# Where a gate is multiplied in, and which queue copies a key: a two-block transformer kernel on one core

## The chip, the cores and the metric

The kernel runs on one core of a Trainium2 chip. The metric is the time of one execution in microseconds of device time: 2701.52 us as the median of three runs, from 2699.83 to 2702.96. A core has a matrix engine (PE in the profile; its weight loads are PEld), a vector engine (DVE), a scalar engine (ACT), GpSimd (POOL) and a sync engine (SP) that issues DMAs. Each engine works through its own list of instructions strictly in order. POOL can issue DMAs as well: these run on a queue of their own, `software_dynamic` in the profile, while those of SP run on `hardware_dynamic`. POOL does not read PSUM, the memory into which the matrix engine writes.

## The reference

Two blocks are computed in float32. The first has a hybrid mixer (dilated attention and an mLSTM), a cross attention and a mixture of 16 experts over 512 tokens. The second has two layers over two streams, the 512 latent tokens `x` and 256 context tokens `xc`, with one set of weights for both. Cut to what matters here:

```python
for l in range(DEPTH_2):                      # 2 layers
    ctx_out = l < DEPTH_2 - 1                 # the context stream is carried on only after layer 0
    sh1, sc1, g1, sh2, sc2, g2 = split(silu(c) @ w_ada[l] + b_ada[l])            # latent
    sh1c, sc1c, g1c, sh2c, sc2c, g2c = split(silu(c_ctx) @ w_ada[l] + b_ada[l])  # context
    o, oc = token_mixers(modulate(x, sh1, sc1), modulate(xc, sh1c, sc1c), ...)
    x = layer_norm(ALPHA * x + g1 * (o @ w_out[l]), ...)
    x = layer_norm(ALPHA * x + g2 * swiglu(modulate(x, sh2, sc2), ...), ...)
    if ctx_out:
        xc = layer_norm(ALPHA * xc + g1c * (oc @ w_out[l]), ...)
        xc = layer_norm(ALPHA * xc + g2c * swiglu(modulate(xc, sh2c, sc2c), ...), ...)
```

The gates `g1`, `g2` and their context forms are vectors of 1024 numbers, one for each output column. So `g * (o @ W)` can be had in two ways: the gate multiplies the columns of W, or it multiplies the product. `token_mixers` holds a neighbourhood attention (NA, 6 heads), a gated linear attention (GLA) and a grouped-query attention (GQA, 2 key heads).

## The kernel before

Products are made of float32 numbers split into two parts: every weight chunk (128 partitions x 1024 numbers, 512 KB) is loaded by SP into `raw`, rounded by ACT into `w_h` (line 350), and DVE writes the rest `w_l = raw - w_h` (line 351). The matrix engine then does three products for each pair of tiles (lines 340 to 344). `wchunk` (line 383) is that chain. If it is given a `row`, POOL multiplies `raw` by it in place first, at line 387, between the landing of the load and ACT.

`proj_tok` (line 394) walks over column halves of 512 and over chunks of a weight, holds one PSUM tile (`pj`) for each 128 tokens, and calls `evac` for each tile at the end. In `out_proj` (line 2076) and `ffn` (line 2097) `evac` adds the PSUM tile onto the residual `x` on DVE (lines 2088 and 2107). The context stream has two token tiles (`nt` = 2), the latent stream four. In the context's layer 0 the gates go into the weights with `row=`: 8 chunks of `w_out` with `g1b`, 22 chunks of the second FFN weight with `g2b`. For latents, `g1b` multiplies the PSUM tile in `out_proj` (lines 2084 to 2087), and `g2b` goes into the weights of the FFN (22 chunks in each of two layers).

The order of the work: the first block runs until about 520 us. Then come the 16 experts, and beside them, as a foreground with the experts pumped in between, the context's layer 0 (to about 1200 us). A context stream has its own small rings (two `raw` buffers, two split buffers, two `pj` tiles; line 1184). Then the context's layer 1, which gives only keys, values and states, then the two latent layers, about 1290 to 2000 us and 2000 to 2707 us. The program is handed to a scheduler that sets the order on each engine at build time; nothing is reordered on the chip.

In attention each key tile needs a second copy of its rows on the other 64 partitions. `dup_k` (line 530) makes four DMAs of 64 partitions for each key tile, all issued by SP: `nak_h`, `nak_l` for NA (called through `stack_k` at line 1590, three pairs of heads per layer) and `gak_h`, `gak_l` for GQA (line 1790). In a latent layer of 512 tokens one such copy moves 128 KB. POOL issues there the loads of the NA bias tiles, `nab` (line 1621), each when the tile's earlier content has been read, and ACT negates them on landing (line 1622). POOL also computes part of the rotary embedding, `gu` (line 1763).

Of the kernel before, what the change touches and what calls it, by code (L numbers as in the profile page):

```python
# [9 lines left out]
F32 = mybir.dt.float32  # L10
# [5 lines left out]
OP = mybir.AluOpType  # L16
# [4 lines left out]
P = 128  # L21
# [11 lines left out]
ALPHA = (2.0 * 2) ** 0.25  # L33
# [202 lines left out]
def f32(ap):  # L236
    return ap.bitcast(F32)
# [22 lines left out]
class Kern:  # L260
# [259 lines left out]
        for h in range(2):  # L520
            self.split(HL(vd(dst[0:64, h]), vd(dst[64:128, h])), vs(ps[64 * h:64 * h + 64]), scale)

    def stack_k(self, k, ps):

        for h in range(2):
            r = slice(64 * h, 64 * h + 64)
            self.split(k[r, h], ps[r])
        self.dup_k(k)

    def dup_k(self, k):  # L530
        for t in (k.hi, k.lo):
            for h in range(2):
                self.nc.sync.dma_start(out=f32(t[64 - 64 * h:128 - 64 * h, h]), in_=f32(t[64 * h:64 * h + 64, h]))

    def scores(self, sc, q, segs):

# [1048 lines left out]
    def na_kq(self, f, l, hT, T, W, lat, full, pool, g, d):  # L1585

        nc = self.nc
        blk = lambda t: t.rearrange("p (b r c) -> p b r c", b=4, c=16)
        k = g["k"] = self.hl_tile(pool, [P, 2, T], "nak", f"nak{f % 2}")
        yield from self.feat_pieces(hT, T, W[:, 384 + f * P:384 + (f + 1) * P], lambda ps: self.stack_k(k, ps[:, :T]))  # L1590
        if not lat:
            d["na_k"].append(self.spill(k, f"nakc{l}{f}"))
        if not full:
            return
        q = g["q"] = pool.tile([P, 2, T], F32R, name="naq", tag=f"naq{f % 2}")

        def ev_q(ps):
            if not lat:
                return self.stack_q(q, ps[:, :T], 0.125)

            for h in range(2):
                t = q[0:64, h], q[64:128, h]
                src = ps[64 * h:64 * h + 64].rearrange("p (r b c) -> p b r c", b=4, c=16)
                nc.scalar.activation(blk(t[0]), src, AF.Copy, scale=-0.125)
                for b in range(4):
                    bs = slice(b * P, (b + 1) * P)
                    nc.vector.scalar_tensor_tensor(out=t[1][:, bs].rearrange("p (r c) -> p r c", c=16), in0=src[:, b],
                                                   scalar=-0.125, in1=f32(t[0][:, bs]).rearrange("p (r c) -> p r c", c=16),
                                                   op0=OP.mult, op1=OP.subtract)
        yield from self.feat_pieces(hT, T, W[:, f * P:(f + 1) * P], ev_q)  # L1610
# [89 lines left out]
    def gqa(self, l, hT, T, W, ctxd, full, d, keep, pool, between, woven):  # L1700


        nc, A = self.nc, self.A
        nt = T // P
        lat = ctxd is not None
# [20 lines left out]
        kS = self.hl_tile(keep, [P, 2, T], "gak")  # L1726
        if full:
            qS = keep.tile([P, 3, 2, T], F32R, name="gaq")
        if lat:
# [4 lines left out]
            for w, nm in ((qw, "q"), (kw, "k")):  # L1734
# [6 lines left out]
                for bb in range(2):  # L1741
                    for aa in range(2):
                        nc.gpsimd.tensor_tensor(out=t4[:, :, aa, bb, :], in0=s4[:, :, aa, bb, :],
                                                in1=w4[:, aa, 1 - bb, :].unsqueeze(1).to_broadcast([P, 4, 16]), op=OP.mult)
                tabs.append((tcs, tsn))
        for i in range(nt):
            t = sq()
            nc.vector.tensor_tensor(out=t, in0=qk[:, i], in1=r[:, i, :].unsqueeze(2).to_broadcast([P, nh, 64]), op=OP.mult)
            f = pool.tile([P, nh, 64], F32, name="gf", tag="gf", bufs=2)
            if lat:  # L1750
                u = pool.tile([P, nh, 64], F32, name="gu", tag="gu", bufs=1)
            for h0, h1, w, ti in ((0, nq, qw, 0), (nq, nh, kw, 1)):
                n = h1 - h0
# [3 lines left out]
                if lat:  # L1757
# [4 lines left out]
                    for bb in range(2):  # L1762
                        nc.gpsimd.tensor_tensor(out=u5[:, :, :, bb, :], in0=s5[:, :, :, 1 - bb, :],
                                                in1=t5[:, :, bb, :].unsqueeze(1).to_broadcast([P, n, 2, 16]), op=OP.mult)
# [3 lines left out]
            f, t = (t, f) if lat else (f, t)  # L1768
# [16 lines left out]
            for h in range(2):  # L1785
# [1 line left out]
                if full:  # L1787
                    self.split(HL(qS[0:64, :, h, ts], qS[64:128, :, h, ts]), tp[r2, 0:384].rearrange("p (k t) -> p k t", t=P))
                self.split(kS[r2, h, ts], tp[r2, (nb - 1) * P:nb * P])
        self.dup_k(kS)  # L1790
        vs = lambda t, hh, j: t[:, j, 64 * hh:64 * hh + 64]
        if not lat:
            d["ga_k"], d["ga_v"] = self.spill(kS, f"gakc{l}"), self.spill(v, f"gavc{l}")
# [267 lines left out]
    def behind_input(self, hT, pool, works):  # L2061

        t = pool.tile([P, 1], F32, name="bhd", tag="bhd", bufs=1)
        with self.tc.issue_after(self.nc.gpsimd.tensor_copy(t, f32(hT.lo[:, KT - 1, T1 - 1:T1])).ins):
            for f in works:
                f()

    def call(self, f):
        if f is not None:
            f()  # L2070
# [5 lines left out]
    def out_proj(self, l, oT, nt, x, g1b, pool, tile_done):  # L2076

        nc = self.nc
        W = self.A["w_out_2"][l]
        stats = {}  # L2080

        def ev(i, c0, n, ps):
            s = slice(c0, c0 + n)
            if nt == 4:
                t = pool.tile([P, 512], F32, name="gps", tag="gps", bufs=1)
                nc.vector.tensor_tensor(out=t, in0=ps, in1=g1b[:, s], op=OP.mult)
                ps = t
            nc.vector.scalar_tensor_tensor(out=x[:, i, s], in0=x[:, i, s], scalar=ALPHA, in1=ps[:, :n], op0=OP.mult, op1=OP.add)
            self.ln_stats(stats, x, i, c0)
            if c0 + n == D:  # L2090
                return tile_done(i, stats[i])
        if nt < 4:
            return self.proj_tok(oT, nt, W, lambda *a: self.call(ev(*a)), row=g1b)
        self.proj_tok(oT, nt, W[:, 0:512], ev)
        self.proj_last(oT, nt, W, ev, pool, KT, None, (512,))

    def ffn(self, l, hT, T, x, g2b, pool, tile_done):

        nc, A = self.nc, self.A
        nt = T // P  # L2100
        Wi, Wo = A["w_ffn_in_2"][l], A["w_ffn_out_2"][l]
        nf = FF // P
        stats = {}

        def ev(i, c0, n, ps):
            s = slice(c0, c0 + n)
            nc.vector.tensor_tensor(out=x[:, i, s], in0=x[:, i, s], in1=ps[:, :n], op=OP.add)  # L2107

        def ev_last(i, c0, n, ps):
            ev(i, c0, n, ps)  # L2110
            self.ln_stats(stats, x, i, c0)
            if c0 + n == D:
                return tile_done(i, stats[i])
        f0, begun = 0, []
        for fg in (4, 4, 4, 4, 2, 4):
            gT = self.hl_tile(pool, [P, 4, T], "wk", bufs=3 if nt == 4 else 2)
            if f0 == 0 and nt == 4:
                begun = self.in_halves(hT, T, [Wi[:, c:c + P] for c in (0, FF, P)], lambda: self.sc("fab"))
            for f in range(fg):
                ab = []  # L2120
                for z in (0, FF):
                    if begun:
                        ab.append(begun.pop(0))
                        continue
                    c0 = z + (f0 + f) * P
                    w = self.wchunk(Wi[:, c0:c0 + P], KT, P)
                    ab.append(self.sc("fab")[:, 0:T])
                    self.mm3(ab[-1], [(w[:, k, :], hT(k)) for k in range(KT)])
                s = pool.tile([P, T], F32, name="fs", tag="fs", bufs=2)
                nc.scalar.activation(s, ab[0], AF.Silu)  # L2130
                nc.vector.tensor_tensor(out=s, in0=s, in1=ab[1], op=OP.mult)
                self.split(gT[:, f, :], s)
            rows = Wo[f0 * P:(f0 + fg) * P, :]
            f0 += fg
            if f0 < nf or nt < 4:
                self.proj_tok(lambda k: gT[:, k, :], nt, rows, ev if f0 < nf else lambda *a: self.call(ev_last(*a)), kt=fg, row=g2b)
            else:
                self.proj_last(lambda k: gT[:, k, :], nt, rows, ev_last, pool, 4, g2b, (0, 512), lag=2)

# [228 lines left out]
```

## Time and profile before

| what | value |
|---|---|
| median of three runs | 2701.52 us |
| profiled execution, own time | 2709.36 us |
| its span, first to last instruction | 2707.6 us |
| PE, DVE, ACT, POOL busy | 93%, 64%, 47%, 15% |
| mean granted PE clock | 0.963 of full speed |

The profile shows one execution. Busy shares are averages over stages with different limits, so a stage is read by itself with the view of stretches, and a wait by the view that says which instruction ended it. Matmuls overlap each other, so the time of one in a row is longer than its share of the engine. `[1.31 <-DVE w_l L351]` at the end of a row says that the engine had been idle for 1.31 us and that the DVE instruction of line 351 that writes `w_l` let it go.

### The profile page before, as it was taken

How to read it: one execution, taken by the hardware profiler on the slowest of the kernel's cores; microseconds unless marked ns; L12 is line 12 of the kernel's file. 1: busy time of each engine (PE TensorE's matmuls, PEld its weight loads, DVE VectorE, ACT ScalarE, POOL GpSimd, SP SyncE). 2: the span in 40 equal slices, each digit the busy share in tenths (PEclk: the TensorE clock that was granted, in tenths of full speed). 3: DMA queues.
4: the chain of work that ended last, by engine and by line, in shares of the span. 5: the costliest groups of instructions: out<-in, count | busy, mean ns of one | idle time of the engine just before them, and what ended most of it. 6: DMA issues, size and time to landing. Idle time of an engine off the chain costs nothing. (4 is left out here: it accounts for less than half of the span.)

```text
span 2707.6 us, 35926 instructions
## 1 busy us (share of the span) xinstructions
PE 2515.4 (93%) x13176; PEld 1963.8 (73%) x13176; DVE 1725.2 (64%) x3117; ACT 1281.9 (47%) x2389; POOL 418.7 (15%) x304
## 2 busy tenths in 40 slices
PE   8999899798889999988998999999989899999997
PEld 5547575676667888877786588888868666888886
DVE  3346646797687787778786665444567776644446
ACT  4344444576655555556656642222266574422221
POOL 1100000201022121022220023111141200411101
PEclk9999899899999999998999999999989999999999
DMA  7765357588777888767254123333323524233331
GB/s 276 208 203 160 117 192 244 159 268 282 250 241 234 268 276 276 252 222 220 81 156 137 69 87 122 96 94 94 104 86 96 146 82 133 71 101 93 94 93 63
DMA packets 355157, 436.54 MB, mean 161 GB/s; under 512 B 20384, under 2 KB 228128, under 8 KB 354976
## 3 DMA queue, kind: packets, MB, share of 16 engines
q1 hardware_dynamic: 350560, 416.90, 49.1%
q0 software_dynamic: 4416, 17.30, 1.8%
q8 instruction: 105, 1.72, 0.3%
q14 instruction: 76, 0.62, 0.1%
HBM read 387.21 MB, written 38.01 MB: 157 GB/s over the span
## 5 line engine op out<-in xcount | busy, mean ns | idle before, releaser
L351 DVE TENSOR_TENSOR w_l<-raw,w_h 128x1024 fp32r<-128x1024 f32 (+2 forms) x530 | 714.5, 1359 | 465.8 <-ACT w_h L350 456.6
L350 ACT CAST w_h<-raw 128x1024 fp32r<-128x1024 f32 (+2 forms) x530 | 527.5, 1007 | 855.6 <-PE pj L343 272.2
L343 PE MATMUL fab<-hTf_h,w_h 128*128 128x512 f32 (+1 forms) x1104 | 386.2, 351 | 4.1 <-ACT hTf_h L514 3.4
L343 PE MATMUL fab<-hTf_h,w_l 128*128 128x512 f32 (+1 forms) x1104 | 386.7, 351 | 0.5 <-DVE w_l L351 0.4
L343 PE MATMUL fab<-hTf_l,w_h 128*128 128x512 f32 (+1 forms) x1104 | 386.2, 350 | 0.2
L387 POOL TENSOR_TENSOR raw<-raw,g2b 128x1024 f32<-128x1024 f32 x66 | 172.3, 2617 | 708.5 <-DMA raw<-in_w_ffn_out 615.1
L343 PE MATMUL pj<-w_l,hT_h 128*128 128x512 f32 (+3 forms) x608 | 229.8, 379 | 14.1 <-DVE w_l L351 14.1
L343 PE MATMUL pj<-w_h,hT_h 128*128 128x512 f32 (+3 forms) x608 | 222.2, 378 | 14.9 <-ACT w_h L350 9.9
L343 PEld LDWEIGHTS fab<-hTf_h,w_h 128*128 128x128 f32 x1104 | 208.9, 190 | 37.2 <-ACT hTf_h L514 4.5
L343 PEld LDWEIGHTS fab<-hTf_h,w_l 128*128 128x128 f32 x1104 | 209.2, 190 | 32.8 <-DVE w_l L351 1.2
L343 PEld LDWEIGHTS fab<-hTf_l,w_h 128*128 128x128 f32 x1104 | 209.2, 190 | 32.2 <-DVE hTf_l L515 0.6
L343 PE MATMUL pj<-w_h,hT_l 128*128 128x512 f32 (+3 forms) x608 | 225.0, 372 | 0.0
L343 PE MATMUL pj<-w_h,wk_h 128*128 128x512 f32 x376 | 148.5, 401 | 7.9 <-DVE x L2107 4.9
L343 PEld LDWEIGHTS pj<-w_h,hT_h 128*128 128x128 f32 x608 | 118.6, 197 | 45.8 <-ACT w_h L350 13.4
L343 PEld LDWEIGHTS pj<-w_l,hT_h 128*128 128x128 f32 x608 | 120.5, 198 | 42.4 <-DVE w_l L351 18.3
L343 PE MATMUL pj<-w_l,wk_h 128*128 128x512 f32 x376 | 150.0, 400 | 1.1 <-DVE w_l L351 0.9
L343 PE MATMUL pj<-w_h,wk_l 128*128 128x512 f32 x376 | 147.3, 399 | 1.2 <-DVE wk_l L351 1.2
L343 PE MATMUL pf<-hT_h,w_h 128*128 128x512 f32 (+3 forms) x376 | 133.4, 356 | 10.2 <-DVE nak_l L351 3.1
L343 PEld LDWEIGHTS pj<-w_h,hT_l 128*128 128x128 f32 x608 | 120.3, 198 | 22.0 <-issue 5.2
L343 PE MATMUL pf<-hT_h,w_l 128*128 128x512 f32 (+3 forms) x376 | 131.2, 350 | 0.0
L343 PE MATMUL pf<-hT_l,w_h 128*128 128x512 f32 (+3 forms) x376 | 131.2, 350 | 0.0
L577 ACT COPY pT<-ptp 128x512 f32<-128x512 f32 (+3 forms) x184 | 88.5, 497 | 53.5 <-PE ptp L575 52.4
(598 smaller groups left out, 4840.7 us busy)
## 6 DMA issues: line engine op xcount, KB each, us to landing
raw<-in_w SPq DMA_DIRECT2D x192, 512.0 KB
raw<-in_w_ffn_in SPq DMA_DIRECT2D x132, 512.0 KB
raw<-in_w_ada SPq DMA_DIRECT2D x96, 512.0 KB
raw<-in_w_in SPq DMA_DIRECT2D x76, 512.0 KB
raw<-in_w_ffn_out SPq DMA_DIRECT2D x66, 512.0 KB
raw<-in_w_out SPq DMA_DIRECT2D x32, 512.0 KB
yd<-ysb SPq DMA_DIRECT2D x16, 512.0 KB
raw<-in_w_in SPq DMA_DIRECT2D x16, 384.0 KB
```

The lines of the kernel that those rows point to most:

```text
L343: self.nc.tensor.matmul(out, lhsT=l, rhs=r, start=first and k == 0 and i == 0, stop=last and k == n - 1 and i == 2, **kw)
L350: nc.scalar.copy(out=hl.hi, in_=src)
L351: nc.vector.tensor_sub(out=hl.lo, in0=src, in1=f32(hl.hi))
L387: self.nc.gpsimd.tensor_tensor(out=raw, in0=raw, in1=row.unsqueeze(1).to_broadcast([P, kt, n]), op=OP.mult)
L577: nc.scalar.copy(out=pT()[:, slice(b0, b0 + bb), ts], in_=tp[:, :bb * P].rearrange("p (b t) -> p b t", t=P))
```

## The change

Two things are moved. In the context's layer 0 the gates no longer multiply weight chunks: `out_proj` multiplies the PSUM tile for both streams, and `ffn` does it for the context alone. For that a new function `times` has DVE write `ps * g` to a tile `gps` in SBUF, of which there is one. And the copies of the latent keys, in NA and in GQA, are issued by POOL; those of the context stay with SP.

```diff
-    def stack_k(self, k, ps):
+    def stack_k(self, k, ps, eng=None):
...
-        self.dup_k(k)
-
-    def dup_k(self, k):
+        self.dup_k(k, eng)
+
+    def dup_k(self, k, eng=None):
         for t in (k.hi, k.lo):
             for h in range(2):
-                self.nc.sync.dma_start(out=f32(t[64 - 64 * h:128 - 64 * h, h]), in_=f32(t[64 * h:64 * h + 64, h]))
+                (eng or self.nc.sync).dma_start(out=f32(t[64 - 64 * h:128 - 64 * h, h]), in_=f32(t[64 * h:64 * h + 64, h]))
...
-        yield from self.feat_pieces(..., lambda ps: self.stack_k(k, ps[:, :T]))
+        yield from self.feat_pieces(..., lambda ps: self.stack_k(k, ps[:, :T], nc.gpsimd if lat else None))
...
-        self.dup_k(kS)
+        self.dup_k(kS, nc.gpsimd if lat else None)
...
+    def times(self, ps, g, pool):
+        t = pool.tile([P, 512], F32, name="gps", tag="gps", bufs=1)
+        self.nc.vector.tensor_tensor(out=t, in0=ps, in1=g, op=OP.mult)
+        return t
...
         def ev(i, c0, n, ps):                                        # out_proj
             s = slice(c0, c0 + n)
-            if nt == 4:
-                t = pool.tile([P, 512], F32, name="gps", tag="gps", bufs=1)
-                nc.vector.tensor_tensor(out=t, in0=ps, in1=g1b[:, s], op=OP.mult)
-                ps = t
-            nc.vector.scalar_tensor_tensor(out=x[:, i, s], in0=x[:, i, s], scalar=ALPHA, in1=ps[:, :n], op0=OP.mult, op1=OP.add)
+            nc.vector.scalar_tensor_tensor(out=x[:, i, s], in0=x[:, i, s], scalar=ALPHA, in1=self.times(ps, g1b[:, s], pool),
+                                           op0=OP.mult, op1=OP.add)
...
-            return self.proj_tok(oT, nt, W, lambda *a: self.call(ev(*a)), row=g1b)
+            return self.proj_tok(oT, nt, W, lambda *a: self.call(ev(*a)))
...
         def ev(i, c0, n, ps):                                        # ffn
             s = slice(c0, c0 + n)
+            if nt < 4:
+                ps = self.times(ps, g2b[:, s], pool)
             nc.vector.tensor_tensor(out=x[:, i, s], in0=x[:, i, s], in1=ps[:, :n], op=OP.add)
...
-                self.proj_tok(lambda k: gT[:, k, :], nt, rows, ev if ..., kt=fg, row=g2b)
+                self.proj_tok(lambda k: gT[:, k, :], nt, rows, ev if ..., kt=fg, row=g2b if nt == 4 else None)
```

On POOL, in the stretch of the experts and the context's layer 0 (`hg` gathers an expert's tokens, `x` is the layer norm's gain and shift), the difference begins:

```order
 L1957 TENSOR_TENSOR glD<-gla_b_4377 128x256
-L1421 DMA hg<-hd,idx 128x1024 x2
-L387 TENSOR_TENSOR raw<-raw,g1b 128x1024 x4
-L1421 DMA hg<-hd,idx 128x1024 x3
-L387 TENSOR_TENSOR raw<-raw,g1b 128x1024 x4
+L1421 DMA hg<-hd,idx 128x1024 x6
+L2078 TENSOR_TENSOR x<-x,lng 128x1024
+L2079 TENSOR_TENSOR x<-x,lnb 128x1024
 L1421 DMA hg<-hd,idx 128x1024
```

The 8 multiplies by `g1b`, and further on the 22 by `g2b`, are gone; gathers and layer norm stay.

On DVE, where the first column half of the second FFN group of the context is evacuated (`es` is an expert's activation, `egT_l` its transposed rest), it read before

```order
L1438 TENSOR_TENSOR es<-es,h_8732 128x512
L351 TENSOR_TENSOR w_l<-raw,w_h 128x1024 x2
L2107 TENSOR_TENSOR x<-x,pj 128x512 x2
L351 TENSOR_TENSOR egT_l<-gtp,egT_h 128x512
L351 TENSOR_TENSOR w_l<-raw,w_h 128x1024 x5
L2107 TENSOR_TENSOR x<-x,pj 128x512 x2
```

and reads now

```order
L1438 TENSOR_TENSOR es<-es,h_8736 128x512
L351 TENSOR_TENSOR w_l<-raw,w_h 128x1024 x2
L2070 TENSOR_TENSOR gps<-pj,g2b 128x512
L2111 TENSOR_TENSOR x<-x,gps 128x512
L351 TENSOR_TENSOR w_l<-raw,w_h 128x1024
L2070 TENSOR_TENSOR gps<-pj,g2b 128x512
L351 TENSOR_TENSOR egT_l<-gtp,egT_h 128x512
L2111 TENSOR_TENSOR x<-x,gps 128x512
L2070 TENSOR_TENSOR gps<-pj,g2b 128x512
L2111 TENSOR_TENSOR x<-x,gps 128x512
```

Each evacuation has become two instructions. The first of them reads the PSUM tile, the second does not, and other work may stand between the two tiles of a pair.

On POOL, in the latent layer 0 after the third `gu` of four, the list was two rows of `gu` and then four bias loads; now it is

```order
L533 DMA nak_l<-nak_l 64x512
L533 DMA nak_h<-nak_h 64x512
L533 DMA nak_l<-nak_l 64x512
L1763 TENSOR_TENSOR gu<-gsq,tsq 128x12x16 x2
L1763 TENSOR_TENSOR gu<-gsq,tsk 128x4x16 x2
L533 DMA gak_h<-gak_h 64x512
L533 DMA gak_l<-gak_l 64x512
L1621 DMA nab_13179<-in_nabias 128x768
L533 DMA gak_h<-gak_h 64x512
L533 DMA gak_l<-gak_l 64x512
L533 DMA nak_h<-nak_h 64x512
```

Behind these rows three more copies stand ahead of the second bias load, one ahead of the third and three ahead of the fourth. In the latent layers the matrix engine's own list is the same as before, row for row.

## Rows read from the trace of the kernel before

**Rows 1.** The page's head: busy us by engine (share of the span) xinstructions.

```profile
PE 2515.4 (93%) x13176; PEld 1963.8 (73%) x13176; DVE 1725.2 (64%) x3117; ACT 1281.9 (47%) x2389; POOL 418.7 (15%) x304
```

**Rows 2.** Stretches: start:end, length, busy us by engine (instructions), clock, DMA share, GB/s.

```profile
600.00:820.00 220.00, 180.87 (x848) 137.51 (x847) 167.39 (x238) 139.32 (x223) 37.58 (x18) 0.92 0.78 257
820.00:1200.00 380.00, 362.32 (x2072) 311.97 (x2072) 293.39 (x308) 210.03 (x261) 66.66 (x29) 0.98 0.78 254
1700.00:1900.00 200.00, 200.00 (x858) 160.96 (x858) 84.71 (x84) 48.75 (x58) 27.31 (x11) 1.00 0.33 95
```

**Rows 3.** Groups of POOL, 600 to 1200 us: count, busy us, mean ns, idle before.

```profile
L387 POOL TENSOR_TENSOR raw<-raw,g2b 128x1024 f32<-128x1024 f32 x22 | 58.5, 2664 | 215.7 <-DMA raw<-in_w_ffn_out 156.1 <-DVE w_l L351 37.1 <-DVE wk_l L351 19.7
L387 POOL TENSOR_TENSOR raw<-raw,g1b 128x1024 f32<-128x1024 f32 x8 | 20.0, 2509 | 51.8 <-DMA raw<-in_w_out 21.0 <-issue 15.6 <-DMA nak_h<-nak_h 15.2
```

**Rows 4.** Groups of DVE in the same stretch, shapes kept apart.

```profile
L351 DVE TENSOR_TENSOR w_l<-raw,w_h 128x1024 fp32r<-128x1024 f32 x250 | 336.4, 1366 | 112.6 <-ACT w_h L350 108.8 <-PE fab L343 2.7
...
L2107 DVE TENSOR_TENSOR x<-x,pj 128x512 f32<-128x512 f32 x24 | 15.8, 677 | 2.2 <-PE pj L343 2.2
L351 DVE TENSOR_TENSOR wk_l<-fs,wk_h 128x256 fp32r<-128x256 f32 x22 | 15.1, 685 | 0.5 <-ACT wk_h L350 0.5
```

**Rows 5.** Timelines of POOL and DVE: start, us, instruction, idle before.

```profile
1005.54 2.84 POOL L387 TENSOR_TENSOR raw<-raw,g2b 128x1024 f32<-128x1024 f32 x1 [2.75 <-DMA raw<-in_w_ffn_out]
...
883.88 1.22 DVE L351 TENSOR_TENSOR w_l<-raw,w_h 128x1024 fp32r<-128x1024 f32 x1 [1.32 <-ACT w_h L350]
...
996.28 13.17 DVE L351 TENSOR_TENSOR w_l<-raw,w_h 128x1024 fp32r<-128x1024 f32 x6 [1.10 <-ACT w_h L350]
```

**Rows 6.** One tile's instructions: `wk_l`, 600 to 1200 us, least/median/most ns.

```profile
L351 DVE TENSOR_TENSOR wk_l<-fs,wk_h x22: 411/418/2619, 833.0 to 1177.4; 128x256 fp32r<-128x256 f32 x22
```

**Rows 7.** Timeline of PE: first, one amid, and last of the idle times counted.

```profile
639.46 0.50 PE L343 MATMUL h<-w_l,ehT_h 128*128 128x512 f32 x1 [1.31 <-DVE w_l L351]
...
1009.51 0.50 PE L343 MATMUL h<-w_l,ehT_h 128*128 128x512 f32 x1 [2.08 <-DVE w_l L351]
...
1186.29 0.73 PE L343 MATMUL pj<-w_h,wk_h 128*128 128x512 f32 x2 [2.70 <-ACT w_h L350]
```

**Rows 8.** Waits of ACT and PE, 600 to 1200 us: total, times, longest.

```profile
ACT w_h L350 <- POOL raw L387: 53.6, 21, 6.2
...
PE pj L343 <- DVE x L2107: 4.9, 3, 2.3
```

**Rows 9.** Groups of DVE in the latent evacuation, 1550 to 1620 us.

```profile
L2088 DVE SCALAR_TENSOR_TENSOR x<-x,gps 128x512 f32<-128x512 f32 x8 | 5.5, 691 | 0.2
L2086 DVE TENSOR_TENSOR gps<-pj,g1b 128x512 f32<-128x512 f32 x8 | 5.5, 682 | 3.0 <-PE pj L343 3.0
```

**Rows 10.** Timeline of SP's queue in the latent layer 0.

```profile
1419.95 4.27 SPq L533 DMA_DIRECT2D gak_h<-gak_h  x1
...
1427.66 0.94 SPq L533 DMA_DIRECT2D nak_h<-nak_h  x1
```

**Rows 11.** Timelines of POOL and of ACT there.

```profile
1430.30 0.54 POOL L1621 DMA_DIRECT2D nab<-in_nabias  x1 [11.86 <-DVE nmx L654]
...
1425.67 0.58 ACT L350 CAST nak_h<-pf 64x512 fp32r<-64x512 f32 x1
```

**Rows 12.** Waits of PE and ACT, 1290 to 1560 us, then 2000 to 2260 us.

```profile
PE sc L542 <- DMA nak_h<-nak_h: 0.5, 1, 0.5
...
ACT nab L1622 <- DMA nab<-in_nabias: 10.0, 4, 4.0
...
PE sc L543 <- DMA nak_l<-nak_l: 1.9, 1, 1.9
...
ACT nab L1622 <- DMA nab<-in_nabias: 12.2, 4, 5.0
```

**Rows 13.** POOL's DMAs by line: issue ns least/median/most; `nab`'s landing us.

```profile
DMA to landing us min/median/max: 3.8/5.9/8.2
...
L1421 POOL DMA_INDIRECT hg<-hd,idx x16: 938/1100/1793, 516.8 to 1075.5; - x16
```

More of the change, by code (lines that the diff above doesn't have):

```diff
@@ L1589, in na_kq @@
         k = g["k"] = self.hl_tile(pool, [P, 2, T], "nak", f"nak{f % 2}")
-        yield from self.feat_pieces(hT, T, W[:, 384 + f * P:384 + (f + 1) * P], lambda ps: self.stack_k(k, ps[:, :T]))
+        yield from self.feat_pieces(hT, T, W[:, 384 + f * P:384 + (f + 1) * P], lambda ps: self.stack_k(k, ps[:, :T], nc.gpsimd if lat else None))
         if not lat:
@@ L2135, in ffn @@
             if f0 < nf or nt < 4:
-                self.proj_tok(lambda k: gT[:, k, :], nt, rows, ev if f0 < nf else lambda *a: self.call(ev_last(*a)), kt=fg, row=g2b)
+                self.proj_tok(lambda k: gT[:, k, :], nt, rows, ev if f0 < nf else lambda *a: self.call(ev_last(*a)), kt=fg,
+                              row=g2b if nt == 4 else None)
             else:
```

## Prediction

> **What bounds the kernel now.** I read the page's head first: the matrix engine (PE) is busy 93% of the span, DVE 64%, POOL 15% [rows 1]. A change that touches POOL and DVE can so only pay where PE stands still for them. The view of stretches tells where that is. Between 600 and 1200 us, where the context's layer 0 and the experts run together, PE is busy 180.87 + 362.32 us of 600, so idle for 56.8 us, and its granted clock is 0.92 and 0.98 of full speed [rows 2]. Between 1700 and 1900 us, in the latent FFN, PE is busy for all 200 us at clock 1.00, although POOL works there too [rows 2]: the 44 gate multiplies that stay in the latent FFNs are covered, and so would a saving on them be.
>
> In the stretch from 600 to 1200 us POOL makes 22 + 8 gate multiplies, 58.5 + 20.0 us [rows 3]. They reach PE in two ways. First, ACT waits for the product 21 times, 53.6 us in all [rows 8], and since ACT works in order, the expert chunks behind wait as well. Second, DVE slows down. One `w_l` alone takes 1.22 us [rows 5]. The six from 996.28 us on, with two POOL multiplies in that time (one stands in the rows), take 13.17 us instead of 7.3 [rows 5]. Over the stretch the mean is 1.366 us over 250 [rows 4], and `wk_l` goes from a median of 0.418 to 2.619 us at most, mean 0.685 over 22 [rows 4, 6].
>
> The rows show that, and the Trainium skill names a cause (SBUF — State Buffer, "SBUF: two separate sides"): a DVE operation with two SBUF inputs and a GpSimd operation share a port pair that one of them holds for its whole length. The trace agrees: 0.418 plus nearly one multiply is the 2.619 of rows 6.
>
> **What goes.** 30 multiplies on POOL, 78.5 us, on an engine nobody needs otherwise: worth nothing by themselves. On DVE the lengthening goes: 250 x (1.366 - 1.22) = 36.5 us and 22 x (0.685 - 0.418) = 5.9 us, together 42.4 us. What of it PE feels I took from its idle times: of those above 0.3 us there are 41 in the stretch, 54.4 us; I followed each back from releaser to releaser. 14 of them lead within five steps to a DVE instruction that overlaps a gate multiply, or to ACT waiting for one: 21.5 us, the first at 639.46 (1.31 us), one amid at 1009.51 (2.08), the last at 1186.29 (2.70) [rows 7]. The clock adds to it: 220 x 0.08 + 380 x 0.02 = 25.2 us of PE time are lost to the lower of its two levels, 1.2 GHz, which follows stretches with such idle times [rows 2]. I give the 14 their share of the idle time, 21.5 / 56.8 = 0.38, so 9.5 us. The gain is then at most 31.0 us; at least it is nothing, if other waits take all the places.
>
> **What comes.** 28 evacuations of the context (2 tiles x 2 halves in `out_proj`, 2 x 2 x 6 groups in the FFN) get a multiply from PSUM of 0.682 us: 19.1 us of DVE. The addition behind it costs 0.691 instead of 0.677 us [rows 4, 9]. DVE so wins 42.4 - 19.1 - 0.4 = 23 us in the stretch. But the new time lies in a sensitive place. PE needs the second PSUM tile back, and this one is now read one multiply and one addition later: 14 column halves x (0.682 + 0.691) = 19.2 us if PE waited every time; nothing if expert products stand between, as they mostly do, and less than nothing if the shorter `w_l` ahead bring DVE to the tile earlier. Before, PE waited for `x` 3 times at 24 FFN evacuations, 4.9 us [rows 8]. I take 3 us, near the lower end, since these three waits came while DVE was late from the multiplies.
>
> ACT no longer waits for POOL but straight for the load, and each `raw` buffer of the context comes free about a multiply earlier, so loads start earlier. Behind them are the experts' loads on the same queue; the DMA share of 0.78 leaves room [rows 2].
>
> Of the 31.0 us I count two thirds, 20.7, since a closed gap often only brings the next wait of ACT or DVE to light; with the 3 us, 18 us less.
>
> **The key copies.** Per latent layer 16 copies move from SP to POOL: 32 in all. SP was held up at one of them for 4.27 us and so issued NA's next key only at 1427.66 us [rows 10], and PE waited for key copies 0.5 us in one layer and 1.9 in the other [rows 12]: 2.4 us to be had, no more, since the weight loads behind SP have no row of PE waiting for them there. What the issue costs on POOL the trace shows for other DMAs only: 0.54 us for a bias load [rows 11], up to 1.793 for a gather [rows 13]; 32 of them are 17 to 57 us of POOL in two layers. It is covered as long as nobody waits for POOL. What stands behind a copy in POOL's list is `gu` and the bias loads; ACT waits for the bias already, 10.0 and 12.2 us [rows 12]. The second bias load stands behind six copies now. It was let go at 1430.30, while ACT had rounded the last key half at 1425.67 + 0.58 = 1426.25 [rows 11]: 4 us, in which the last two copies have room, and the earlier ones are gone by then. Landing takes 3.8 to 8.2 us for a bias tile of three times the size [rows 13]; the copies start up to 7 us earlier than on SP. I count 2 us less, the trace's own 2.4 being the upper end.
>
> **Sum.** 18 + 2 = 20 us off the profiled execution's 2709.36: 2689.4. The median of the runs lies 7.84 us below that execution, so I forecast 2681.5 us; with the gain between 10 and 33 us (31.0 + 2.4), 2668 to 2692.
>
> **Rivals.**
> A, the gaps move. Context and experts are fed by one stream of loads, 255 GB/s or so, 2 us per chunk of 512 KB, and ACT and DVE serve it in order; where a POOL wait goes, PE waits for the next chunk instead, and the 19.2 us at the PSUM tiles come out in full. For it: 27 of the 41 idle times have nothing to do with POOL. Against it: DMA is at 0.78, DVE at 460.8 of 600 us, neither full [rows 2]. 31.0 - 19.2 leaves 12 at best, and less as gaps move: 2696 to 2707 us, about 2701. Chance 0.17.
> B, POOL becomes late in the latent layers, and the kernel is slower. In front of the four bias loads of a layer stand 2, 6, 1 and 3 copies, 24 in both layers. If the keys come due just when the bias does, each copy delays the bias, ACT stands at it in order, and PE behind ACT. At the gather's median of 1.1 us that is 26 us, at its 1.793 us 43 us [rows 13]; beyond 20 / 24 = 0.83 us each it eats the gain. That gives 2708 to 2725 us, say 2712. For it: ACT's long waits for the bias [rows 12]. Against it: the 4 us above. Chance 0.13.
> The Trainium skill speaks for B (SBUF — State Buffer, the box on "DVE blocks DMA"): a DMA issued by GpSimd has its descriptors written by GpSimd, which a DVE operation can shut out; it gives 620 ns alone and 3100 ns overlapped, by which 24 copies would be an estimated 74 us. The gathers' spread from 0.938 to 1.793 us [rows 13] agrees in kind, not in size.
> C, more than that: without the 14 gaps PE runs through, and the whole 25.2 us of clock come back with the 21.5: 47 us, 2655 us. Against it: the other 27 gaps stay. Chance 0.07.
>
> **Chances.** Forecast 0.63, A 0.17, B 0.13, C 0.07. What a measurement of this kernel can tell from no change is about 0.2%, 5.4 us. Forecast and C are faster, with a bit of A: 0.72. Most of A and a little of B are no change: 0.16. Slower is the rest of B and a little of A: 0.12. The range for 8 in 10 runs from 2660, which leaves out the most of C, to 2704, which leaves out most of B.
>
> **What would show it.** Right: in the context's stretch no row of ACT waiting for POOL's `raw`, `w_l` at 1.22 to 1.25 us in the mean, PE idle around 35 to 40 us instead of 56.8 over the same work, and the first `gu` of the latent layer 0 some 18 us earlier. Wrong, by A: `pj` waiting for `gps` or `x` at most column halves, or as much idle time behind loads. Wrong, by B: ACT waiting over 20 us per layer for `nab`, with the copies' issues directly ahead of it on POOL. The key copies were right if PE no longer waits for `nak`. If the stretches behind 1290 us differ by more than 4 us in length, my reading of the copies was wrong.

## The result: about 33 us faster, and the profile after

| | before | after |
|---|---|---|
| median of four runs | 2700.68 us (2694.79 to 2702.96) | 2669.71 us (2659.42 to 2670.60) |
| profiled execution | 2709.36 us | 2669.79 us |
| mean granted clock there | 0.963 | 0.970 |

The ratio is 0.9878, 95% interval 0.9855 to 0.9902: 26 to 39 us less, 33 as the best value. The forecast was 20 us less and 2681.5 us, range 2660 to 2704. The direction and the range held; the gain came out at 1.65 times the forecast. Where it came from is read from the profiled executions, which lie 39.6 us apart: more than the 33, since the profiled execution of before lies 8.7 us above its median. The experiment e2 below shows how much that is: up to 1300 us its kernel has the same lists of instructions as before, and its profiled execution reached the place at 1300 us 7.7 us earlier. So some 8 of the 39.6 us belong to that one execution and not to the change.

The stretches of the kernel after, in the columns of [rows 2]. The context's layer 0 and the experts, 600 to 1200 us before, now end at 1166 us, 34 us earlier; the third row is the whole of that stretch, the fourth goes on to the place that stood at 1300 us.

```profile
600.00:820.00 220.00, 188.02 (x929) 147.16 (x928) 171.95 (x254) 147.50 (x232) 18.27 (x10) 0.95 0.83 275
820.00:1166.00 346.00, 339.62 (x2005) 297.11 (x2003) 270.62 (x319) 203.84 (x254) 6.24 (x6) 1.00 0.82 267
600.00:1166.00 566.00, 527.64 (x2932) 444.27 (x2930) 442.57 (x573) 351.34 (x486) 24.50 (x16) 0.98 0.82 270
600.00:1264.60 664.60, 612.22 (x3409) 517.03 (x3408) 514.90 (x728) 413.13 (x604) 51.94 (x39) 0.97 0.81 265
```

At 1200 us before and at 1166 us now PE has done the same number of matmuls since the start. The stretch took PE 180.87 + 362.32 = 543.19 us before [rows 2] and takes 527.64 us now. So the 34 us have two parts. PE is busy for 15.6 us less, with the granted clock at 0.95 and 1.00 instead of 0.92 and 0.98. And PE is idle for 566 - 527.64 = 38.4 us instead of 56.8, which is 18.4 us less; its idle times of 0.3 us or more are 27 instead of 41, and their sum 36.1 us instead of 54.4. That is the number of idle times that the prediction had put down to the gates, 14; that they are the same ones isn't shown by the count.

Groups of DVE between 600 and 1166 us, as [rows 4]:

```profile
L351 DVE TENSOR_TENSOR w_l<-raw,w_h 128x1024 fp32r<-128x1024 f32 x253 | 308.2, 1231 | 101.4 <-ACT w_h L350 100.5
...
L2070 DVE TENSOR_TENSOR gps<-pj,g2b 128x512 f32<-128x512 f32 x24 | 16.4, 684 | 2.4 <-PE pj L343 2.1
L2111 DVE TENSOR_TENSOR x<-x,gps 128x512 f32<-128x512 f32 x24 | 16.4, 683 | 0.2
...
L351 DVE TENSOR_TENSOR wk_l<-fs,wk_h 128x256 fp32r<-128x256 f32 x22 | 9.2, 417 | 0.0
...
L2070 DVE TENSOR_TENSOR gps<-pj,g1b 128x512 f32<-128x512 f32 x4 | 2.7, 676 | 0.0
```

`w_l` is down from 1.366 to 1.231 us in the mean and `wk_l` from 0.685 to 0.417, as worked out; the 28 new multiplies cost the 19.1 us of DVE that were counted. What PE waits for there, in all, times and longest:

```profile
PE gtp L1441 <- DVE es L1438: 7.4, 4, 2.7
PE sc L542 <- ACT pc L661: 6.3, 2, 5.4
PE yps L343 <- ACT egT_h L350: 6.1, 6, 2.8
...
PE pj L343 <- DVE w_l L351: 0.9, 2, 0.5
...
PE pj L343 <- DVE gps L2070: 0.2, 1, 0.2
```

The new multiply holds PE up for 0.2 us in all, and the three waits for `x` of [rows 8] have no row any more. What remains belongs for the most part to the experts' own chains (`es`, `egT`) and to the context's attention (`pc`). ACT has no row of a wait for POOL's `raw` left, where it had 53.6 us.

Two marks in POOL's timeline show where the time went off: the latent layer 0's first `glD`, at 1299.15 us before, and its first `gu`, at 1384.43 us before.

```profile
1263.73 1.04 POOL L1957 TENSOR_TENSOR glD<-gla_b 128x512 f32<-128x512 f32 x1 [21.02 <-DVE gla_b L1861]
...
1349.03 2.61 POOL L1763 TENSOR_TENSOR gu<-gsq,tsq 128x192 f32<-128x192 f32 x2 [19.16 <-DVE gsq L1748]
```

Both come 35.4 us earlier. From the `gu` to the end it was 1323.2 us and is 2668.0 - 1349.03 = 1319.0: the latent layers win another 4.2 us. There ACT waits for `nab` 10.7 and 9.8 us in the two layers (10.0 and 12.2 before, [rows 12]), and PE waits for no key copy.

```profile
ACT nab L1622 <- DMA nab<-in_nabias: 10.7, 3, 4.3
...
ACT nab L1622 <- DMA nab<-in_nabias: 9.8, 3, 3.6
```

The copies take POOL this long (least, median, most ns, by tile):

```profile
L533 POOL DMA_DIRECT2D nak_h<-nak_h x12: 516/518/565, 1359.9 to 2129.7; - x12
L533 POOL DMA_DIRECT2D nak_l<-nak_l x12: 516/524/728, 1364.5 to 2130.5; - x12
...
L533 POOL DMA_DIRECT2D gak_h<-gak_h x4: 528/545/648, 1379.3 to 2100.2; - x4
L533 POOL DMA_DIRECT2D gak_l<-gak_l x4: 526/704/881, 1380.4 to 2101.4; - x4
```

### The profile page after: what moved, and what is told of

Read it like the earlier page. It is cut to its first block, busy times and chain, and to the rows that moved or that the text cites. A ratio compares the mean times of both kernels' runs of the same rounds, so it can differ in the third digit from the quotient of the medians.

```text
span 2668.0 us, 35928 instructions
## 1 busy us (share of the span) xinstructions
PE 2497.6 (94%) x13176; PEld 1956.3 (73%) x13176; DVE 1705.8 (64%) x3145; ACT 1282.5 (48%) x2389; POOL 359.9 (13%) x306
## 4 chain that ended last, share of the span: by engine, by line
PE 45%; DVE 5%; ACT 3%; issue 1%; POOL 1%; DMA 1%; DVEq 0%; ACTq 0%; POOLq 0%
PE fab L343 18%; PE pj L343 17%; PE oat L635 3%; PE pf L343 2%; PE ptp L575 1%; PE sc L542 1%; PE glG L1981 1%; PE sc L543 1%; DMA nab<-in_nabias 1%; DVE w_l L351 1%; POOL x L2079 0%; PE tp L500 0%; ACT pga L661 0%; POOL x L2078 0%; ACT ht L508 0%
## 5 line engine op out<-in xcount | busy, mean ns | idle before, releaser
L351 DVE TENSOR_TENSOR w_l<-raw,w_h 128x1024 fp32r<-128x1024 f32 (+2 forms) x530 | 680.0, 1290 | 454.1 <-ACT w_h L350 446.2
L387 POOL TENSOR_TENSOR raw<-raw,g2b 128x1024 f32<-128x1024 f32 x44 | 115.1, 2625 | 493.8 <-DMA raw<-in_w_ffn_out 452.4
```

Source lines behind the costliest of these rows:

```text
L351: nc.vector.tensor_sub(out=hl.lo, in0=src, in1=f32(hl.hi))
L387: self.nc.gpsimd.tensor_tensor(out=raw, in0=raw, in1=row.unsqueeze(1).to_broadcast([P, kt, n]), op=OP.mult)
```

## The experiments

The prediction had named two ways in which POOL's multiply reaches PE: ACT's wait for the product (theory W) and the lengthening of DVE's instructions beside it (theory L). The trace of before can't tell them apart, since both stand at the same places. Line numbers shift by three in kernels with lines added. Each ratio is against runs of the kernel before on the same chip; "the first `glD`" is the mark above. The mark counts from the start of the execution, and POOL's first gather `hg`, up to which all these kernels do the same, stands at 513.0 us (e8) to 519.6 us (after); so the column behind it counts from that gather. The last two columns are of the one profiled execution each: before and e2, with the same instructions up to the mark, differ by 8.5 us there.

| kernel | median, us | ratio, 95% interval | first `glD`, us | first `hg` to first `glD`, us | first `gu` to end, us |
|---|---|---|---|---|---|
| before | 2701 | 1 | 1299.2 | 782.4 | 1323.2 |
| after | 2669.7 | 0.9878 (0.9855 to 0.9902) | 1263.7 | 744.1 | 1319.0 |
| e1_gates_only | 2671.9 | 0.9884 (0.9862 to 0.9906) | 1264.6 | 747.6 | 1322.3 |
| e2_keys_only | 2693.2 | 0.9973 (0.9959 to 0.9988) | 1291.4 | 773.9 | 1314.4 |
| e3_idle_pool | 2706.3 | 1.0013 (0.9999 to 1.0026) | 1296.1 | 781.7 | 1318.0 |
| e4_no_gates | 2664.0 | 0.9860 (0.9836 to 0.9883) | 1255.7 | 740.5 | 1316.8 |
| e5_one_input | 2682.1 | 0.9926 (0.9907 to 0.9945) | 1264.4 | 750.1 | 1323.7 |
| e7_idle_one_input | 2677.1 | 0.9921 (0.9907 to 0.9935) | 1264.1 | 750.0 | 1316.0 |
| e8_wait_one_input | 2667.8 | 0.9881 (0.9865 to 0.9896) | 1258.0 | 745.1 | 1315.8 |

One reservation holds for several rows. The scheduler sets the order anew for each kernel, and PE's list stands apart from the changed kernel's at 465 (e3), 248 (e7), 1936 (e4) and 2228 (e8) of its 13176 places, e5's from that of the kernel before at 1811. A difference of a few microseconds between these kernels can be the order's; no run separates that.

**The two parts, each alone.** In e1 PE's order is that of the changed kernel, in e2 that of the kernel before.

```diff
# e1, against the changed kernel
-self.stack_k(k, ps[:, :T], nc.gpsimd if lat else None)
+self.stack_k(k, ps[:, :T])
-self.dup_k(kS, nc.gpsimd if lat else None)
+self.dup_k(kS)
# e2: these lines of the change alone, put into the kernel before
```

> The changed kernel with the latent key copies back on SP's queue; PE's order is that of the changed kernel. Theory G (the gates make the gain, the copies 2 to 5 us, as the stretches behind 1300 us differ by 3.5 us in the two traces): 28 us less than before, 2672 us, PE waits for nak copies again. Rival K (the copies make a third or more of the gain, because SP, free of them, issues loads earlier): 20 us less than before or fewer, 2680 us or more.

> The kernel before with the latent key copies on POOL's queue alone; the gates stay multiplied into the weights, PE's order is that of before. Theory G: 2 to 5 us less than before, 2697 us, no PE wait for nak, stretch 600 to 1200 us unchanged. Rival K: 10 us or more less, 2690 us. Rival B of the prediction (copies late behind POOL's work or ahead of the bias loads): 5 us or more above before, 2706 us, with ACT waiting longer for nab.

Measured: the gates alone take 31 us off (25 to 37), the copies alone 7 (3 to 11). Theory G holds for the gates, rival K isn't borne out, and rival B is refuted: copies on POOL make nothing slower. They are worth more than either text had as its best value, though. In e1 PE waits for key copies again, in layer 0 and then in layer 1:

```profile
PE sc L542 <- DMA nak_h<-nak_h: 1.3, 1, 1.3
...
PE sc L543 <- DMA nak_l<-nak_l: 1.5, 1, 1.5
PE sc L542 <- DMA nak_h<-nak_h: 0.7, 1, 0.7
```

In e2 no such row is left. The last column of the table separates the two kinds without an overlap: kernels with the copies on SP (before, e1, e5) take 1322.3 to 1323.7 us from the first `gu` to the end, those with the copies on POOL 1314.4 to 1319.0, on the mean of the six 6.4 us less. The waits themselves are 2.4 us [rows 12] to 3.5 (e1). The other half is in PE's busy time. From the first `gu` to the end, before and then e2:

```profile
1384.43:2707.60 1323.17, 1252.20 (x6237) 990.95 (x6235) 778.56 (x1382) 533.04 (x1038) 235.66 (x139) 0.97 0.33 100
...
1377.05:2691.40 1314.35, 1245.68 (x6237) 991.15 (x6235) 771.89 (x1382) 533.21 (x1038) 252.48 (x171) 0.98 0.33 100
```

For the same 6237 matmuls PE is busy 6.5 us less here, with the granted clock at 0.98 instead of 0.97, and idle 2.3 us less. Between the mean of the three kernels with the copies on SP and that of the six with them on POOL it is 3.7 us of busy time and 2.7 us of idle time. Why the clock rises by that much for so little idle time was not isolated.

**POOL beside DVE, but nobody waits for it.** POOL again multiplies every one of the 30 chunks, into a tile that nobody reads; the real gates stay in PSUM.

```diff
 raw = self.wraw(src, kt, n)
+if idle is not None:                                  # g1b, g2b of the context
+    self.nc.gpsimd.tensor_tensor(out=self.spare, in0=raw, in1=idle..., op=OP.mult)
```

> The changed kernel, and for each of the context's 30 gate weight chunks POOL also makes the old multiply from the loaded chunk into a spare tile that nobody reads: POOL works beside DVE as before, but ACT rounds straight from the load and waits for no product. Theory L (what went is the lengthening of DVE under POOL's multiplies): w_l again at 1.33 us or more in the mean in the context's stretch, half of the gain or more lost, 2685 to 2695 us. Theory W (what went is ACT's wait for the product, with the expert chunks behind it): within 6 us of the changed kernel, 2670 to 2676 us, even with w_l lengthened.

Measured: 2706.3 us, the whole gain gone. Theory W, that the wait was the gain, falls. DVE's `w_l` between 600 and 1300 us:

```profile
L351 DVE TENSOR_TENSOR w_l<-raw,w_h 128x1024 fp32r<-128x1024 f32 x258 | 356.5, 1400 | 102.6 <-ACT w_h L350 102.3
```

And PE's largest waits in that stretch are the ones for `w_l` (8.8 and 7.6 us in the kernel before):

```profile
PE pj L343 <- DVE w_l L351: 16.4, 13, 3.7
PE h L343 <- DVE w_l L351: 8.5, 8, 3.9
```

ACT has no row of a wait for this product. Theory L had expected half of the gain or more to go, 2685 to 2695 us; all of it went. Two things add to the lengthening of before here: `w_l` is longer still (1.400 us in the mean against 1.366 [rows 4]), and DVE carries the new multiplies as well.

**A POOL operation that lengthens DVE less.** In the kernel before, POOL multiplies the context's chunks by the constant 1, with one SBUF input; the context's gates are left out.

```diff
-self.nc.gpsimd.tensor_tensor(out=raw, in0=raw, in1=row..., op=OP.mult)
+if plain:                                             # the context's chunks
+    self.nc.gpsimd.tensor_scalar(out=raw, in0=raw, scalar1=1.0, scalar2=None, op0=OP.mult)
+else:
+    self.nc.gpsimd.tensor_tensor(out=raw, in0=raw, in1=row..., op=OP.mult)
```

> The kernel before, but for the context's 30 gate chunks POOL multiplies the loaded chunk by the constant 1 (one input from SBUF) instead of by the gate row (two), so the context's gates are left out; ACT still waits for POOL's product. Theory L (only the lengthening of DVE counts): if w_l beside this operation stays at 1.22 to 1.25 us, the time comes near the changed kernel, 2665 to 2680 us, although ACT waits for POOL 15 to 30 us; if w_l is lengthened as by the two-input multiply (mean over 1.33), 2695 to 2705 us. Theory W (ACT's wait counts): 2690 us or more with w_l at 1.25 or less.

Measured: 2682.1 us, with ACT waiting for POOL 30.8 us. The operation is even longer than the multiply that it replaces (600 to 1280 us):

```profile
L388 POOL TENSOR_SCALAR raw<-raw 128x1024 f32<-128x1024 f32 x30 | 89.1, 2971 | 267.8 <-DMA raw<-in_w_ffn_out 159.2 <-DVE w_l L351 39.5 <-DMA raw<-in_w_out 35.7
```

But it lengthens DVE far less: 600 to 1200 us, 49 `w_l` that overlap it (45 by more than 0.1 us) are longer than 1.22 us by 7.9 us in all, with 50 us of overlap; 30 beside the two-input multiply were longer by 31.9 us, with 43 us of overlap. One case, POOL's row and then DVE's:

```profile
906.00 3.54 POOL L388 TENSOR_SCALAR raw<-raw 128x1024 f32<-128x1024 f32 x1 [13.24 <-DVE w_l L351]
```

```profile
906.83 1.26 DVE L351 TENSOR_TENSOR wk_l<-fs,wk_h 128x256 fp32r<-128x256 f32 x1
908.02 1.21 DVE L351 TENSOR_TENSOR w_l<-raw,w_h 128x1024 fp32r<-128x1024 f32 x1
```

The `wk_l` that began first takes three times its 0.418 us; the `w_l` behind it lies wholly inside the POOL operation and takes its usual time. All the cases go by that pattern. Beside the two-input multiply, each of the 18 `w_l` that began while it ran ended 1.08 or 1.09 us behind it: DVE was shut out until the multiply was nearly over. Of 21 `w_l` wholly inside a one-input operation six took 1.21 to 1.23 us, and the other fifteen, of 1.37 to 2.06 us, all ended 0.65 to 0.66 us before the operation did: DVE was shut out in its first part alone and free for the last 1.9 us of some 2.8. Theory L's number, 2665 to 2680 us, was missed by 2 us: the mean of `w_l` stayed at 1.288 us over 260, between the two levels, so that neither theory's condition was met as written, and the copies of this kernel are still on SP.

**The same operation in the changed kernel, without and with ACT's wait.**

```diff
# e7, against e3
-self.nc.gpsimd.tensor_tensor(out=self.spare, in0=raw, in1=idle..., op=OP.mult)
+self.nc.gpsimd.tensor_scalar(out=self.spare, in0=raw, scalar1=1.0, scalar2=None, op0=OP.mult)
# e8: the same into raw itself, so that ACT must wait
+self.nc.gpsimd.tensor_scalar(out=raw, in0=raw, scalar1=1.0, scalar2=None, op0=OP.mult)
```

> As e3_idle_pool (gates in PSUM, POOL works from each of the 30 loaded chunks into a spare tile that nobody reads, ACT waits for none of it), but POOL's operation has one SBUF input (times the constant 1) instead of two. In e5_one_input such an operation lengthened 45 w_l beside it by 7.9 us in all, where 30 beside the two-input multiply in the kernel before were lengthened by 31.9 us. Theory L (the lengthening of DVE costs, at 0.8 us or so for each us): 8 to 12 us of lengthening, 2674 to 2680 us, some 28 us under e3_idle_pool. Rival H (not the lengthening, but that POOL holds the chunk's buffer longer, and so delays the loads): 2695 us or more, near e3_idle_pool.

> The changed kernel, with POOL multiplying each of the 30 loaded chunks in place by the constant 1 (one input) before ACT rounds it: the output is the reference's, ACT waits for POOL again, and DVE is lengthened little. Against e7_idle_one_input it prices ACT's wait alone. Theory L: within 5 us of e7_idle_one_input, 2674 to 2682 us. Theory W in part (e5_one_input stood 12 us above the changed kernel while ACT waited 30.8 us for POOL): 8 to 18 us above e7_idle_one_input, 2684 to 2695 us.

e7 came as theory L expected, 25 us under e3 by the ratios for one input less on POOL: the lengthening is what costs, and rival H (the chunk held longer) falls as the main cause. e8 bears most directly on the wait. ACT waits for POOL again, 600 to 1300 us:

```profile
ACT w_h L350 <- POOL raw L387: 37.8, 17, 5.0
```

and the time is that of the changed kernel, 0.9881 against 0.9878. So theory W in part, 2684 to 2695 us, is wrong too: 38 us of ACT waiting for POOL cost nothing that can be measured, where the two intervals together leave some 9 us open. A little of the wait does reach PE: its waits for `w_h` sum to 7.0 us before, 7.1 in e5 and 3.8 in e8 between 600 and 1300 us, and to 1.3 to 1.8 us in the kernels where ACT doesn't wait for POOL (after, e3, e7). That e8 is faster than e7, by 9 us in the medians and below theory L's 2674 to 2682 us, was expected by nobody. In the traces POOL's operation overlaps 55 `w_l` in e7 and 38 in e8, since in e8 a chunk's `w_l` can't start before POOL is done with that chunk, and that is 8.7 against 5.9 us of lengthening; but e7's profiled execution (2668.72 us) was the fastest of its five, so this trace can't show what the others lost, and the two kernels' orders differ. It stays open.

**The price of the new multiplies.**

```diff
-in1=self.times(ps, g1b[:, s], pool)
+in1=ps[:, :n]                                         # context only
-if nt < 4:
-    ps = self.times(ps, g2b[:, s], pool)
```

> The changed kernel without the context's gates at all (neither multiply; the context's layer 0 adds ungated projections): it prices the 28 new DVE multiplies from PSUM. My term of 3 us for them: 2664 to 2670 us, 0 to 5 us less than the changed kernel. Rival (PE pays them nearly in full, 19 us, as the second PSUM tile comes back late): 2650 to 2655 us.

This kernel leaves the context's gates out. Measured: 0.9860 against 0.9878, 5 us less, and the intervals overlap. That agrees with the term of 3 us and refutes 19, as the two intervals together allow some 14 at most.

**Covered in the latent FFN?** The first five of six weight groups there are gated in PSUM as well.

```diff
-if nt < 4:
+if nt < 4 or f0 < nf:
     ps = self.times(ps, g2b[:, s], pool)
...
-row=g2b if nt == 4 else None)
+row=None)
```

> The changed kernel with the latent FFN's first five groups gated in PSUM too (36 POOL multiplies, some 94 us, go; 80 DVE multiplies of 0.68 us from PSUM come). My reading (PE is busy all the time there, so DVE's lengthening and POOL's work are covered): 2666 to 2674 us, within 4 us of the changed kernel. Rival P (PE waits for the PSUM tiles read later by a multiply, four at a time): 10 us or more above it, 2680 us. Rival L2 (the lengthening costs there too): 5 us or more below it, 2665 us or less.

Measured: 2666.4 us, 0.9866 (0.9839 to 0.9893): no difference from the changed kernel that can be told. Between 1700 and 1850 us the changed kernel's row is the first, this kernel's the second:

```profile
1700.00:1850.00 150.00, 150.00 (x645) 120.67 (x644) 65.96 (x64) 37.74 (x45) 25.60 (x10) 1.00 0.32 95
```

```profile
1700.00:1850.00 150.00, 150.00 (x645) 120.67 (x644) 68.16 (x81) 37.91 (x45) 0.00 (x0) 1.00 0.33 96
```

PE does the same 645 matmuls in both and never stops, while `w_l` falls from 1.479 to 1.223 us in the mean. From the first `gu` to the end the 154 `w_l` of 1024 columns and the FFN's 44 `wk_l` are together 41 us shorter. The kind of lengthening that cost some 31 us in the context's stretch costs nothing that can be told where PE is full.

**Other POOL operations that lengthen DVE.** v1 and v2 move the context's affine behind its first layer norm, and combine's multiply by the final gain, from POOL to DVE; v4 is v1, v2 and e6 together, v5 also moves the latent affines.

```diff
-self.nc.gpsimd.tensor_tensor(out=out, in0=t, in1=g, op=OP.mult)       # affine: v1 context, v5 all
+eng.tensor_tensor(out=out, in0=t, in1=g, op=OP.mult)                  # eng = nc.vector; the addition alike
-nc.gpsimd.tensor_tensor(out=xs[i], in0=xs[i], in1=g, op=OP.mult)      # v2
+nc.vector.tensor_tensor(out=xs[i], in0=xs[i], in1=g, op=OP.mult)
```

> The changed kernel with the context's affine behind its first layer norm (4 POOL operations, 11.0 us at 794 to 808 us) on DVE. Theory L goes on: two w_l of 2.76 and 2.46 us and two hTf_l of 2.81 and 2.54 us there fall to 1.22 and 0.68, 6.9 us less, against 4 x 1.23 = 4.9 us more on DVE; PE's three idle times there (2.7, 2.0 and 3.4 us) shrink: 3 us less, 2667 us. Rival (DVE's work in that place counts whoever does it): 2670 to 2675 us, no less than the changed kernel.

> The changed kernel with combine's four multiplies by the final gain (POOL, 2.36 to 3.37 us each, 10.9 us at 1206 to 1235 us) on DVE. Theory L: hT_l of 2.42 us and a rqz of 2.34 us there fall to 0.68 and 0.15, PE's idle times of 2.0, 0.7 and 2.0 us shrink: 3 us less, 2667 us. Rival (4 x 1.23 us of DVE in its place): 2670 to 2675 us.

> The changed kernel with v1_affine_dve, v2_gfin_dve and e6_latent_gates together. If the small gains of the three (2.0, 2.6 and 3.3 us in the medians, none clear alone) are real and add up: 2660 to 2663 us. If they are chance: 2666 to 2671 us.

> v4_all_three with the latent layers' affines on DVE as well (24 more operations go from POOL to DVE at about 1.22 us, 29 us; in the changed kernel POOL's lengthen some ten w_l by about 20 us there). Theory L, with PE busy nearly all the time there: 1 to 3 us under v4_all_three, from PE's idle times of 0.4 and 1.7 us behind w_l of 3.4 us in latent layer 1. Rival (they stand in DVE's order in front of what PE waits for): 4 us or more above v4_all_three.

Measured: v1 2667.7 us (0.9876), v2 2667.1 (0.9879), v4 2663.2 (0.9854, 0.9838 to 0.9871), v5 2659.7 (0.9848, 0.9835 to 0.9862). In v1 the mechanism is as expected at its place: `hTf_l` there falls from 2.672 to 0.678 us and PE's idle times over 0.3 us in the 37 us around it from 12.3 to 6.9 us. In time neither v1 nor v2 can be told from the changed kernel, and whether the small gains add up in v4 isn't settled either. v5 has the lowest median of all, 10 us under the changed kernel's (8 by the ratios); its interval still overlaps the changed kernel's, so that it beats both is settled against before, and only likely against after.

## Why the prediction was right, and what it mis-sized

- **What bounds the stretch.** Right. PE stood still in the context's stretch and the gain came from there: 35.4 of the profiled 39.6 us lie before 1300 us (28 of them against e2's execution), and e6 shows the cover in the latent FFN that was read from [rows 2].
- **"They reach PE in two ways."** Wrong. ACT's wait, 53.6 us of [rows 8] and the largest row in sight, was worth nothing that these runs can tell: e8 brings 38 us of it back at no measured cost, e3 takes it away and wins nothing. DVE's lengthening, with nobody waiting, brings the whole loss back in e3. A likely reason, not tested by itself: ACT has room (210 of 380 us busy in [rows 2]'s second stretch), and PE waits for `w_l`, which comes after `w_h`. The forecast didn't suffer from it, because the sum was taken from PE's own idle times, whichever of the two ways led there. Nor does it hang on a miscount in the example: beside the six `w_l` from 996.28 us stood three multiplies (995.78, 1000.14 and 1005.54 us), not two.
- **The idle time that goes.** 14 idle times with 21.5 us were counted, and two thirds of that as gain. 14 fewer there are, and 18.4 us of idle time less. The discount "since a closed gap often only brings the next wait to light" was too large: as much as 0.86 of the sum came, not 0.67.
- **The clock.** Of the gates' sum this is the term most mis-sized. It was given the same share as the idle times, 0.38 of 25.2 us or 9.5 before the discount, and 15.6 us came. The rows show why a share of the sum does not do: the granted clock lost 25.2 us before, and now 220 x 0.05 + 346 x 0 = 11 us. The clock loss fell by 14 us, more than half, while the idle time fell by a third.
- **What comes, at the PSUM tiles.** 3 us were taken between 0 and 19.2. PE's waits for `gps` are 0.2 us, and e4 prices all 28 multiplies at about 5 us, not distinguishable from 3 or 0. Rival A, that gaps move there, found no support.
- **The key copies.** 2 us with 2.4 as the upper end; e2 measures 7 (3 to 11), and the last column of the table 6. The upper end was taken from the two rows of waiting alone, and the clock, which the gates' sum had, was left out; about half of what came is PE's busy time. The prediction's own sign for this, stretches behind 1290 us that differ by more than 4 us, came true at 4.2 us. The reasoning on `nab` was right: at 0.52 us per copy, under the 0.83 us that B needed, ACT's wait for the bias moved by +0.7 and -2.4 us.
- **The Trainium skill on copies** (SBUF — State Buffer, the box on "DVE blocks DMA" and, for the figure, "A bandwidth-pool intuition that's wrong") spoke for B with 3100 ns per overlapped issue. The Trainium skill gives that figure for an issue beside a DVE `tensor_copy`, a condition that the prediction left out. All 32 copies here overlap DVE at work, but none a `tensor_copy`, and none took longer than 0.881 us; so the price didn't apply to them, and the skill's own case isn't tested here.
- **The Trainium skill on the port pair** (SBUF — State Buffer, "SBUF: two separate sides") says that a DVE operation with two SBUF inputs and a GpSimd operation that reads SBUF exclude each other for a whole instruction. For the two-input multiply the rows agree: `w_l` goes from 1.22 to 3.4 us and ends 1.1 us behind the multiply. For the one-input operation they agree in its first part only: the `wk_l` at 906.83 us was held, and the `w_l` at 908.02 us ran at full speed inside an operation that reads SBUF.

The sum: 31 us for the gates against 18 forecast, 7 for the copies against 2. The one stands at the upper end that the prediction gave it (31.0 us), the other above it (2.4 us), and together they reach the edge of "between 10 and 33 us"; that the time still lay inside is in part luck, and the wide range's lower end, 2660, lay beyond what the mechanism as written allowed.

## What to carry to other kernels

The instruction that waits longest need not be the one that costs: look for the engine that the bound engine waits for, and price a shared cause by an experiment that keeps one of its effects and drops the other (POOL's work with nobody waiting, and the wait without the lengthening). In this kernel a two-input elementwise operation on POOL was paid on DVE as well, at 0.74 us for each us beside a two-input subtraction there; it cost nothing that could be told where PE never stopped. When idle times of PE go, count the granted clock apart: here 14 to 16 of its 25.2 us came back while a third of the idle time went. And before two traces are compared, look how far two executions of the same instructions lie apart, 8.5 us here.

## What the runs showed of the hardware that was not expected

- A one-input POOL operation of 128 x 1024 numbers took 2.97 us in the mean, longer than the two-input multiply at 2.66 [rows 3], and lengthened DVE's subtractions beside it by 0.16 us per us of overlap, against 0.74 for the two-input one.
- `w_l` beside such a one-input operation was at most 2.06 us long in e5, against 3.44 beside the multiply in the kernel before; `wk_l` at most 1.26 us, against 2.62. Both pairs come to the same lengthening, at most 0.84 us for the one-input operation and 2.2 us for the two-input one.
- A copy of a key tile issued from POOL takes 0.52 us of POOL in the median for NA's and 0.55 and 0.70 for GQA's, half to two thirds of a gather's 1.1 us [rows 13].
